# The FFN output projection as pairs of 64-row products in the PE array

## The chip, the core and the metric

The kernel runs on one core of a Trainium2 chip. The metric is the device time of one execution in microseconds (us); lower is better. Each compared time is the median of several executions, and beside them stands one profiled execution, whose trace is what the views of the profile are read from. Engines are named as the profile names them: PE is the matrix engine (PEld its weight loads), DVE and ACT the two engines that do elementwise work and activations, POOL a third one that here does little, and SP the engine that issues most DMAs.

## The reference

The program is a trunk of two layers on one sequence of 256 positions and 1024 channels, all in float32. Each layer has three sub-layers with an RMS norm before and after each: an FFN, a mixer (differential attention beside an mLSTM), and a second FFN. The change touches only the FFN:

```python
def _swiglu(h, w_in, w_out):
    gate, up = jnp.split(h @ w_in, 2, axis=-1)
    return (jax.nn.silu(gate) * up) @ w_out

h = _swiglu(_rmsnorm(x, g[0]), ffn_w_in[l, 0], ffn_w_out[l, 0])
x = x + 0.5 * _rmsnorm(h, g[1])
```

The hidden width is 2816. The input projection is 1024 by 5632, the output projection 2816 by 1024, and there are four FFNs in all.

## The kernel before

The 256 positions are two tiles `t` of 128 rows. The hidden width is cut into 11 chunks `c` of 256. For each chunk three weight pieces of 1 MB come from memory: two for the input projection and one, `wo`, for the output projection. Each half of a piece is split by ACT (line 278, the high part `wh`) and DVE (line 279, the low part `wl`), and a product in near-float32 precision is made of three PE products of the type fp32r: high by high, high by low, low by high (`mm3`, lines 393 to 395).

For a chunk and a tile, `in_piece` fills a PSUM bank `pin` with 24 such products of 128 rows of contraction, 128 stationary columns and 512 moving columns. `ffn_hidden` makes the hidden activations from it (ACT line 256, DVE line 516), `ffn_split` transposes them on PE (line 523, two transposes to a tile and chunk) and splits them into `hh` and `hl`. `out_part(c, t, h, wo)` then adds the chunk to the output: for each half `hf` of the 1024 output columns, 2 blocks `k` of 128 rows of contraction, by 3 products, 12 in all for a tile and chunk. The output of an FFN is held in four PSUM banks `bk`, one for each tile and column half, which are added to over all 11 chunks. So an FFN has 264 output products of 128 rows, and the four FFNs 1056.

The order on PE is set by a scheduler with a cost model, within the dependencies, except from `yield "ending"` (line 614) to `"running"`, where it is the order in which the code issues the instructions. Three chunks' outputs are still pending at the ending (`pend`). There the code issues: the transposes of tile 0 of the last chunk; the output of the oldest pending chunk for tile 0; the transposes of tile 1; the other two chunks for tile 0; `"done"` for tile 0, whose handler `postnorm` normalises the two finished banks and adds them to `x`; two chunks for tile 1; `"next"`, whose handler transposes the new `x` of tile 0 on PE for the next sub-layer (`prenorm`, line 412, 8 transposes); the last chunk for tile 1; and `"done"` for tile 1.

`postnorm` is a chain: ACT squares each bank with a running sum (line 454), DVE adds the two sums (line 438), POOL raises the sum to the power -1/2 (line 401), and DVE scales and adds to `x` in two halves (line 467).

Of the kernel before, what the change touches and what calls it, by code (L numbers as in the profile page):

```python
# [15 lines left out]
F32 = mybir.dt.float32  # L16
# [9 lines left out]
NT = S // P  # L26
# [29 lines left out]
def _pack(inp):  # L56
# [20 lines left out]
    for l in range(L):  # L77
        at = l * PIECES_LAYER
        ffn(at, l, 0)
        at += PIECES_FFN  # L80
        for n, lo in enumerate(MIX_GROUPS):
            a = m_in[l][:, lo:lo + 512].reshape(2, 4, P, 512).transpose(0, 2, 1, 3)
            w[at + 2 * n:at + 2 * n + 2] = a.reshape(2, P, 2048)
        at += 2 * len(MIX_GROUPS)
        w[at:at + 4] = m_out[l].reshape(4, 2, P, D).transpose(0, 2, 1, 3).reshape(4, P, 2048)
        ffn(at + 4, l, 1)
# [41 lines left out]
class _Trunk:  # L128
# [113 lines left out]
    def after(self, ins, others):  # L242

        for o in others:
            self.tc.add_manual_dep(ins.ins, o.ins.name, mybir.DependencyInfo(
                mybir.DependencyClass.NoSync, mybir.DependencyReason.DATA), reason="turn")

    def table(self, name, last=None):

        self.loaded = self.nc.scalar.preload_act_table_set(name)  # L250
        self.after(self.loaded, self.users + ([last] if last else []))
        self.users = []
# [280 lines left out]
    def ffn(self, pre, gi_post):  # L533
        xT, r = pre

        def in_piece(t, kh, pin, w):
            xh, xl = xT[t][kh]
            for k in range(4):
                self.mm3(pin, xh[:, k, :], xl[:, k, :], *self.cols(w, k),
                         start=kh == 0 and k == 0, stop=kh == 1 and k == 3)  # L540

        def out_part(c, t, h, wo):
            hh, hl = h[t]
            for hf in range(2):
                for k in range(2):
                    self.mm3(po[t][hf], hh[:, k, :], hl[:, k, :], *self.cols(wo, 2 * k + hf),
                             start=c == 0 and k == 0, stop=c == NC_FF - 1 and k == 1)

        po, pend = None, []
        if not xT:  # L550

            xT += [[], []]
            pins = [self.bank_bk() for _ in range(NT)]
            self.piece_at = 2
            with self.tc.manual_schedule(engines={mybir.EngineType.PE, mybir.EngineType.Activation, mybir.EngineType.DVE}):
                self.first_chunk(pins, xT)
            self.turns = [[(self.cast, self.split)]]
            for t in range(NT):
                ss = self.small("ss", (P, 2))
                for hf in range(2):  # L560
                    self.after(self.square(t, hf, ss), [self.cast])
                r.append(self.rsqrt_sum(ss, EPS))
            h = [self.ffn_evac(pins[t], r[t]) for t in range(NT)]
            begin = 1
        else:

            w0 = [self.piece(), self.piece()]
            w1 = [self.piece()]
            pa, pa1 = self.bank_pin(), self.bank_pin()
            in_piece(0, 0, pa, w0[0])  # L570
            in_piece(0, 1, pa, w0[1])
            ha = self.ffn_hidden(pa, r[0])
            yield "second"
            in_piece(0, 0, pa1, w1[0])
            ha = self.ffn_split(ha)
            pb = self.bank_pin()
            in_piece(1, 0, pb, w0[0])
            in_piece(1, 1, pb, w0[1])
            yield "running"
            w1.append(self.piece())  # L580
            in_piece(0, 1, pa1, w1[1])
            hb = self.ffn_evac(pb, r[1])
            pend = [(0, [ha, hb], self.piece())]
            pb1 = self.bank_pin()
            ha1 = self.ffn_evac(pa1, r[0])
            in_piece(1, 0, pb1, w1[0])
            in_piece(1, 1, pb1, w1[1])
            po = [[self.bank_bk() for _ in range(2)] for _ in range(NT)]
            for t in range(NT):
                out_part(0, t, *pend[0][1:])  # L590
            pend = []
            h = [ha1, self.ffn_evac(pb1, r[1])]
            begin = 2
        for c in range(begin, NC_FF):
            ws = [self.piece(), self.piece()]
            pend.append((c - 1, h, self.piece()))
            if c == 3:
                g = self.load_gpost(gi_post)
                yield "middle"
            pins = [self.bank_pin() for _ in range(NT)]  # L600
            for kh in range(2):
                for t in range(NT):
                    in_piece(t, kh, pins[t], ws[kh])
            if c == NC_FF - 1:
                break
            h = [self.ffn_evac(pins[t], r[t]) for t in range(NT)]
            if len(pend) == DEFER - 1 or po is None:
                if po is None:
                    po = [[self.bank_bk() for _ in range(2)] for _ in range(NT)]
                cc, hc, wo = pend.pop(0)  # L610
                for t in range(NT):
                    out_part(cc, t, hc, wo)

        yield "ending"
        h = [self.ffn_evac(pins[0], r[0]), None]
        pend.append((c, h, self.piece()))
        out_part(pend[0][0], 0, *pend[0][1:])
        h[1] = self.ffn_evac(pins[1], r[1])
        for p in pend[1:]:
            out_part(p[0], 0, *p[1:])  # L620
        yield "done", po[0], g
        for p in pend[:-1]:
            out_part(p[0], 1, *p[1:])
        yield "next"
        out_part(pend[-1][0], 1, *pend[-1][1:])
        yield "done", po[1], g


# [515 lines left out]
def _trunk(tc, a, out, phases=3 * L):  # L1144
    nc = tc.nc
    with contextlib.ExitStack() as st:
        def pool(name, bufs, **kw):
            return st.enter_context(tc.tile_pool(name=name, bufs=bufs, **kw))

        fill = pool("fill", 1)  # L1150
        fill.tile([P, FILL // 4], F32, name="fill")
        wr, wl, wh, trp, k4 = pool("wr", 3), pool("wl", 7), pool("wh", 7), pool("tr", 6), pool("k4", 6)
        hp, k2, const, ded = pool("hp", 4), pool("k2", 10), pool("const", 1), pool("ded", 1)
        const.tile([P, CFILL // 4], F32, name="cfill")
        pools = (const, wr, wl, wh, trp, k2, k4, ded, hp, pool("sm", 2), pool("ps", 1, space=PSUM))
        tr = _Trunk(tc, a, out, pools)
        tr.x = [tr.const.tile([P, D], F32, name=f"x{t}") for t in range(NT)]
        tr.early = {}
        tr.start()
        tr.users = []  # L1160
        tr.table("silu_and_others")
        tr.half = tr.const.tile([P, 16], F32, name="c_half")
        nc.gpsimd.memset(tr.half, -0.5)
        tr.run(phases)
# [17 lines left out]
```

## Time and profile before

| what | value |
|---|---|
| median of the runs shown | 985.39 us (985.11 to 985.68, 2 runs) |
| the profiled execution | 986.18 us, its span 984.4 us |
| PE busy | 976.0 us, 99% of the span |
| DVE, ACT, POOL busy | 606.4, 528.4 and 27.6 us |
| mean granted PE clock | 0.998 of full speed |
| memory traffic | 177.01 MB read, 181 GB/s over the span |

In the profile a row of a timeline gives the start, the duration, the engine, the line, the operation, the output and input by the program's names, the shape and the count; in brackets stands the idle time before it and what ended it. The shape `128*128 128x512` of a PE product is rows of contraction by stationary columns, then the moving operand. Products are pipelined, so that a PE product lasts longer (0.39 us) than the distance to the next one. The chain of waits gives each piece of work the time by which it put off the end.

### The profile page before, as it was taken

The numbers are of one execution on the slowest core, as the hardware profiler recorded it, in microseconds if no ns is written. First come the engines' busy times: TensorE is split into PE (matmuls) and PEld (weight loads), VectorE is DVE, ScalarE is ACT, GpSimd is POOL, SyncE is SP. The second block draws the span as 40 slices with busy tenths as digits, with TensorE's granted clock in tenths as the row PEclk, the third lists the DMA queues.
The fourth block names the chain that finished last, engine by engine and source line by source line (L and its number), as shares of the span: only waits on it lengthen the run. The fifth ranks groups of instructions, "written<-read, shape, count | busy, mean of one in ns | idle before, by whom it ended". The sixth has DMA issues, their size and how long they took to land.

```text
span 984.4 us, 12032 instructions
## 1 busy us (share of the span) xinstructions
PE 976.0 (99%) x4629; PEld 800.2 (81%) x4629; DVE 606.4 (62%) x863; ACT 528.4 (54%) x869; POOL 27.6 (3%) x51
## 2 busy tenths in 40 slices
PE   9999999999999999999999999999999999999997
PEld 6888888888788888888888888888888888888885
DVE  6755554589867655555485645455888586554542
ACT  7744444477856545444375544444778475544431
POOL 1000000000010000000000000000001000000000
PEclk9999999999999999999999999999999999999999
DMA  8954545336352844464356455443454257544511
GB/s 304 346 217 174 197 169 192 124 129 216 123 196 95 312 167 179 184 239 171 129 207 242 162 188 207 178 163 119 166 207 167 90 205 263 195 171 171 210 48 43
DMA packets 27640, 178.84 MB, mean 182 GB/s; under 512 B 3034, under 2 KB 4186, under 8 KB 6846
## 3 DMA queue, kind: packets, MB, share of 16 engines
q1 hardware_dynamic: 27006, 177.46, 48.9%
q8 instruction: 36, 0.59, 0.2%
q10 hardware_dynamic: 576, 0.61, 0.2%
q14 instruction: 22, 0.18, 0.0%
HBM read 177.01 MB, written 1.05 MB: 181 GB/s over the span
## 4 chain that ended last, share of the span: by engine, by line
PE 99%; DMA 1%; DVE 0%; SPq 0%; ACT 0%; POOLq 0%; issue 0%; DVEq 0%; ACTq 0%
PE pin L393 21%; PE pin L395 20%; PE pin L394 20%; PE bk L393 10%; PE bk L395 10%; PE bk L394 10%; PE ptr L523 2%; PE ptr L805 1%; PE ptr L412 1%; PE bk L1017 1%; PE bk L1057 1%; DMA x<-in_x_dram 1%; PE bk L372 0%; PE bk L370 0%; PE bk L1097 0%; PE bk L371 0%
## 5 line engine op out<-in xcount | busy, mean ns | idle before, releaser
L279 DVE TENSOR_TENSOR wl<-wr,wh 128x1024 fp32r<-128x1024 f32 x324 | 389.4, 1223 | 223.4 <-ACT wh L278 213.7
L278 ACT ACTIVATE wh<-wr 128x1024 fp32r<-128x1024 f32 x324 | 336.5, 1057 | 190.4 <-PE pin L395 102.1
L393 PE MATMUL pin<-wh,th 128*128 128x512 f32 x880 | 349.5, 398 | 0.0
L395 PE MATMUL pin<-wh,tl 128*128 128x512 f32 x880 | 343.4, 391 | 0.0
L394 PE MATMUL pin<-wl,th 128*128 128x512 f32 x880 | 343.3, 390 | 0.0
L395 PEld LDWEIGHTS pin<-wh,tl 128*128 128x128 f32 x880 | 165.2, 188 | 35.2
L393 PEld LDWEIGHTS pin<-wh,th 128*128 128x128 f32 x880 | 165.4, 188 | 33.3 <-ACT vd L1002 0.8
L394 PEld LDWEIGHTS pin<-wl,th 128*128 128x128 f32 x880 | 165.5, 188 | 32.3
L393 PE MATMUL bk<-wh,hh 128*128 128x512 f32 x352 | 140.0, 398 | 0.0
L395 PE MATMUL bk<-wh,hl 128*128 128x512 f32 x352 | 137.6, 393 | 0.0
L394 PE MATMUL bk<-wl,hh 128*128 128x512 f32 x352 | 137.6, 391 | 0.0
L526 ACT ACTIVATE hh<-ptr 128x256 fp32r<-128x256 f32 x88 | 33.2, 377 | 93.3 <-PE ptr L523 75.6
L256 ACT ACTIVATE sil<-pin,rs 128x256 f32<-128x256 f32 x86 | 40.5, 472 | 73.7 <-PE pin L395 69.8
L395 PEld LDWEIGHTS bk<-wh,hl 128*128 128x128 f32 x352 | 66.1, 188 | 13.8
L394 PEld LDWEIGHTS bk<-wl,hh 128*128 128x128 f32 x352 | 66.2, 188 | 12.8
L393 PEld LDWEIGHTS bk<-wh,hh 128*128 128x128 f32 x352 | 66.1, 188 | 12.8
L527 DVE TENSOR_TENSOR hl<-ptr,hh 128x256 fp32r<-128x256 f32 x88 | 37.1, 422 | 54.3 <-ACT hh L526 51.5
L516 DVE SCALAR_TENSOR_TENSOR h<-pin,rs,sil 128x256 f32<-128x256 f32 x86 | 41.2, 480 | 30.2 <-ACT sil L256 30.2
L401 POOL TENSOR_TENSOR rs<-s,c_half 128x1 f32<-128x1 f32 x24 | 13.1, 553 | 774.2 <-DVE s L438 774.2
L523 PEld LDWEIGHTS ptr<-c,h 128*128 128x128 f32 x176 | 24.7, 140 | 11.5
L523 PE MATMUL ptr<-c,h 128*128 128x128 f32 x176 | 33.4, 271 | 0.0
L454 ACT ACTIVATE junk<-bk 128x512 bf16<-128x512 f32 x24 | 14.2, 592 | 31.1 <-PE bk L395 31.1
(179 smaller groups left out, 586.8 us busy)
## 6 DMA issues: line engine op xcount, KB each, us to landing
wr<-in_w_dram SPq DMA_DIRECT2D x162, 1024.0 KB, 4.9
gpost<-in_gpost_dram SPq DMA_DIRECT2D x6, 512.0 KB, 6.2
wr<-in_w_dram SPq DMA_DIRECT2D x2, 512.0 KB, 7.1
wr<-in_w_dram SPq DMA_DIRECT2D x3, 256.0 KB, 5.2
x<-in_x_dram SPq DMA_DIRECT2D x3, 256.0 KB, 5.8
out_dram<-x SPq DMA_DIRECT2D x2, 256.0 KB, 2.1
x<-in_x_dram SPq DMA_DIRECT2D x2, 128.0 KB, 2.7
wr<-in_w_dram ACTq DMA_DIRECT2D x1, 256.0 KB, 3.5
```

The source lines that it names most:

```text
L256: i = self.nc.scalar.activation(*args, **kw)
L278: ia = nc.scalar.activation(hi, raw[:, j], AF.Copy)
L279: iv = nc.vector.tensor_tensor(lo, raw[:, j], hi.bitcast(F32), op=ALU.subtract)
L393: mm(ps, xh, wh, start=start, stop=False)
L394: mm(ps, xh, wl, start=False, stop=False)
L395: mm(ps, xl, wh, start=False, stop=stop)
L401: self.nc.gpsimd.tensor_tensor(r, ss, self.half[:, :width], op=ALU.pow)
L454: return nc.scalar.activation(self.junk_tile(), po[hf], AF.Square, scale=1.0 / (16 if half else 32), accum_out=ss[:, hf:hf + 1])
L516: nc.vector.scalar_tensor_tensor(h, pin[:, 256:512], r, sil, op0=ALU.mult, op1=ALU.mult)
L523: nc.tensor.transpose(ptr[:, k, :], h[:, k * P:(k + 1) * P], self.ident)
L526: nc.scalar.activation(hh, ptr, AF.Copy)
L527: nc.vector.tensor_tensor(hl, ptr, hh.bitcast(F32), op=ALU.subtract)
```

## The change

The 128 rows of contraction of each output product are cut into two halves of 64 rows. A product of the rows 0 to 63 stands in the upper half of the array and one of the rows 64 to 127 in the lower half, and the two that stand side by side belong to different PSUM banks. `rows_of` takes two orders of banks, one for each half of the array, issues the products of both in turn, and so each bank gets its upper and its lower half of the contraction at different times. Where a bank passes from one half of the array to the other, `behind` makes the first product there wait for the last one of the other half, by way of a one-element memset on POOL.

`out_rows` does this for a chunk with all four banks: the upper half of the array goes through tile 0 and then tile 1, the lower half through tile 1 and then tile 0. `out_tile` does it at the ending, for one tile with all three pending chunks: the upper half fills the bank of the first column half and then that of the second, the lower half the other way round. The ending changes with it: both tiles' last hidden activations are made and transposed first, then all of tile 0 follows, and `"next"` now stands before all of tile 1. The pool of `hh` and `hl` has six buffers in place of four.

```diff
+    def behind(self, ins, other):
+        step = self.nc.gpsimd.memset(self.sm.tile([1, 1], F32, tag="turn", name=self.name("turn")), 0.0)
+        for a, b in ((step, other), (ins, step)):
+            self.tc.add_manual_dep(a.ins, b.ins.name, mybir.DependencyInfo(
+                mybir.DependencyClass.Sync, mybir.DependencyReason.DATA), reason="turn")
...
+        def rows_of(orders):
+            for pair in zip(*orders):
+                for half, (t, hf, c, h, wo) in enumerate(pair):
+                    b, rows = 2 * t + hf, slice(half * 64, half * 64 + 64)
+                    for k in range(2):
+                        for lhs, rhs in ((0, 0), (0, 1), (1, 0)):
+                            todo[half].append((b, half, po[t][hf], h[t][lhs][rows, k, :], self.cols(wo, 2 * k + hf)[rhs][rows]))
+                for both in zip(*todo):
+                    for b, half, bank, x, w in both:
+                        i = self.nc.tensor.matmul(bank, x, w, start=last[b] is None, stop=False, skip_group_check=True)
+                        if last[b] and last[b][0] != half:
+                            self.behind(i, last[b][1])
+                        last[b] = half, i
+                for v in todo:
+                    v.clear()
+
+        def out_rows(c, h, wo):
+            p = (c, h, wo)
+            rows_of([[(t, hf, *p) for t, hf in order] for order in
+                     (((0, 0), (0, 1), (1, 0), (1, 1)), ((1, 0), (1, 1), (0, 0), (0, 1)))])
+
+        def out_tile(t, ps):
+            rows_of([[(t, hf, *p) for hf in order for p in ps] for order in ((0, 1), (1, 0))])
+
+        todo, last = [[], []], [None] * 4
...
-                for t in range(NT):
-                    out_part(cc, t, hc, wo)
+                out_rows(cc, hc, wo)
...
         h = [self.ffn_evac(pins[0], r[0]), None]
         pend.append((c, h, self.piece()))
-        out_part(pend[0][0], 0, *pend[0][1:])
         h[1] = self.ffn_evac(pins[1], r[1])
-        for p in pend[1:]:
-            out_part(p[0], 0, *p[1:])
+        out_tile(0, pend)
         yield "done", po[0], g
-        for p in pend[:-1]:
-            out_part(p[0], 1, *p[1:])
         yield "next"
-        out_part(pend[-1][0], 1, *pend[-1][1:])
+        out_tile(1, pend)
...
-        hp, k2, const, ded = pool("hp", 4), pool("k2", 10), pool("const", 1), pool("ded", 1)
+        hp, k2, const, ded = pool("hp", 6), pool("k2", 10), pool("const", 1), pool("ded", 1)
```

In the program's order the 1056 output products are now 2112 of 64 rows. They stand in 140 unbroken runs, and other PE work stands between the runs. In the changed kernel's line numbers, L570 is an output product of 64 rows, L400 to L402 are the products of `mm3`, L530 the transposes of the hidden activations, L419 those of `prenorm`, and L408 the power on POOL.

The first place is PE in the middle of the first FFN, after the output of a chunk for tile 0 (`bk_408` and `bk_409` are the banks of tile 0, `bk_410` and `bk_411` those of tile 1). Before:

```order
L394 MATMUL bk_409<-wl_1_462,hh_393 128x512
L395 MATMUL bk_409<-wh_1_463,hl_394 128x512
L523 MATMUL ptr_520<-c_95,h_518 128x128 x2
L393 MATMUL pin_616<-wh_0_541,th_126 128x512
L394 MATMUL pin_616<-wl_0_540,th_126 128x512
```

and now, at the end of a run and around the next one:

```order
L570 MATMUL bk_410<-wh_1_495,hl_405 128x512
L530 MATMUL ptr_713<-c_95,h_711 128x128 x2
L570 MATMUL bk_408<-wh_1_495,hl_394 128x512
L400 MATMUL pin_814<-wh_0_787,th_126 128x512
L401 MATMUL pin_814<-wl_0_786,th_126 128x512
L402 MATMUL pin_814<-wh_0_787,tl_127 128x512
L400 MATMUL pin_814<-wh_0_787,th_126 128x512
L401 MATMUL pin_814<-wl_0_786,th_126 128x512
L570 MATMUL bk_411<-wh_0_491,hh_404 128x512
L570 MATMUL bk_409<-wh_0_491,hh_393 128x512
```

Transposes and input products of 128 rows now stand between products of 64 rows, and the product into `bk_408` between them has lost its partner of the other half.

The second place is PE at the end of the first FFN, at `"next"`. Before, 24 output products of tile 1 (the last six of them are the first rows here) stand between the last one of tile 0 and the transposes of `x`:

```order
L393 MATMUL bk_411<-wh_0_1491,hh_1440 128x512
L394 MATMUL bk_411<-wl_0_1490,hh_1440 128x512
L395 MATMUL bk_411<-wh_0_1491,hl_1441 128x512
L393 MATMUL bk_411<-wh_1_1495,hh_1440 128x512
L394 MATMUL bk_411<-wl_1_1494,hh_1440 128x512
L395 MATMUL bk_411<-wh_1_1495,hl_1441 128x512
L412 MATMUL ptr_1657<-c_95,x_93 128x128 x4
L412 MATMUL ptr_1668<-c_95,x_93 128x128 x4
L393 MATMUL bk_410<-wh_0_1564,hh_1590 128x512
```

and now:

```order
L570 MATMUL bk_409<-wl_1_1879,hh_1869 128x512
L570 MATMUL bk_408<-wl_1_1879,hh_1869 128x512
L570 MATMUL bk_409<-wh_1_1880,hl_1870 128x512
L570 MATMUL bk_408<-wh_1_1880,hl_1870 128x512
L419 MATMUL ptr_1987<-c_95,x_93 128x128 x4
L419 MATMUL ptr_1998<-c_95,x_93 128x128 x4
L570 MATMUL bk_410<-wh_0_1637,hh_1546 128x512
L570 MATMUL bk_411<-wh_0_1637,hh_1546 128x512
```

The last products of both banks of tile 0 are now the instructions right ahead of the transposes of the `x` that is made from these banks, and all output products of tile 1 stand behind them.

The third place is POOL at the end of the first FFN, with the semaphores that each instruction waits for. Before, the powers of the two tiles' `postnorm` and of the next sub-layer's norms follow each other:

```order
L193 TENSOR_SCALAR c_570<-c_570 128x2
L401 TENSOR_TENSOR rs_177_1628<-s_176_1626,c_half 128x1 [waits DVE_49,Pool_49]
L401 TENSOR_TENSOR rs_192_1701<-s_191_1699,c_half 128x1 [waits DVE_49,Pool_49]
L401 TENSOR_TENSOR rs_197_1713<-s_196_1711,c_half 128x1 [waits DVE_49,Pool_49]
L401 TENSOR_TENSOR rs_214_1819<-s_213_1817,c_half 128x1 [waits DVE_49,Pool_49]
```

and now:

```order
L250 MEMSET turn_1933 1x1 [waits PE_49,Pool_49]
L250 MEMSET turn_1936 1x1 [waits Pool_49]
L250 MEMSET turn_2011 1x1 [waits Pool_49]
L408 TENSOR_TENSOR rs_240_1982<-s_239_1980,c_half 128x1 [waits DVE_49]
L250 MEMSET turn_2048 1x1 [waits PE_49,Pool_49]
L250 MEMSET turn_2051 1x1 [waits Pool_49]
L408 TENSOR_TENSOR rs_258_2097<-s_257_2095,c_half 128x1 [waits DVE_49]
```

Memsets that wait for PE now stand among the powers; the pair ahead of `rs_240` belongs to the change of banks inside tile 0, the pair behind it to that inside tile 1.

More of the change, by code (lines that the diff above doesn't have):

```diff
@@ L547, in out_part @@
                              start=c == 0 and k == 0, stop=c == NC_FF - 1 and k == 1)
+        last = [None] * 4
+        def rows_of(orders):
[20 more added lines that the diff above has]
+        todo, last = [[], []], [None] * 4
         po, pend = None, []
@@ L588, in ffn @@
             po = [[self.bank_bk() for _ in range(2)] for _ in range(NT)]
-            for t in range(NT):
-                out_part(0, t, *pend[0][1:])
+            out_rows(0, *pend[0][1:])
             pend = []
@@ L610, in ffn @@
                 cc, hc, wo = pend.pop(0)
-                for t in range(NT):
-                    out_part(cc, t, hc, wo)
+                out_rows(cc, hc, wo)
         yield "ending"
```

## The prediction

> **What bounds the kernel now.** First the profile's page: the span, PE's busy time, the chain of waits and the output products among the costliest groups.
>
> ```profile
> span 984.4 us, 12032 instructions
> PE 99%; DMA 1%; DVE 0%; SPq 0%; ACT 0%; POOLq 0%; issue 0%; DVEq 0%; ACTq 0%
> L393 PE MATMUL bk<-wh,hh 128*128 128x512 f32 x352 | 140.0, 398 | 0.0
> L395 PE MATMUL bk<-wh,hl 128*128 128x512 f32 x352 | 137.6, 393 | 0.0
> L394 PE MATMUL bk<-wl,hh 128*128 128x512 f32 x352 | 137.6, 391 | 0.0
> ```
>
> PE carries 99% of the chain. Whatever puts PE off puts off the end, and what the other engines do counts only where PE waits for it. The changed products are 3 x 352 = 1056. Their distance is read from a timeline of the first FFN's end: the first of these rows is the last output product of tile 0, the second stands 24 products on.
>
> ```profile
> 185.66 0.39 PE L395 MATMUL bk<-wh,hl 128*128 128x512 f32 x1
> ...
> 191.10 0.39 PE L395 MATMUL bk<-wh,hl 128*128 128x512 f32 x1
> ```
>
> (191.10 - 185.66) / 24 = 0.227 us: the output products cost 1056 x 0.227 = 240 us. Next I looked for 64-row products; the mixer has some. In the chain of waits (start, length of the piece, what):
>
> ```profile
> 247.19 1.09 PE bk L1017 x16
> 248.29 0.89 PE bk L972 x16
> 249.18 0.43 PE pin L393
> 249.61 0.23 PE pin L394
> ...
> 256.70 1.93 PE bk L1017 x16
> 258.63 0.43 PE pin L393
> 259.06 0.24 PE pin L394
> ...
> 270.55 2.68 PE bk L1057 x24
> ```
>
> L972 is 64 rows by 128 columns of plain float32, L1057 the same with 128 rows. 128 rows take 2.68 / 24 = 0.112 us each, 64 rows 0.89 / 16 = 0.056: two really run side by side, a pair in the time of one. But L1017 at 247.19 is as large as L972 and took 1.09, 0.20 more, and the first 128-row product behind each stretch took 0.43 where its neighbours take 0.23. So each change of shape costs PE 0.20 us, in both directions.
>
> **The change part by part.** *Pairs.* 1056 products become as many pairs at best. For two fp32r products of 512 columns side by side there is no row. Nearest in kind is the 128-row one at 0.227; nearest in shape are the L1017 pairs of 256 float32 columns, (1.93 - 0.20) / 8 = 0.216. I take 0.227, because every fp32r row shows it, output and input products alike (0.23 in the chain above), and keep 0.216 as the low end (and 0.233, as much above, for the high). At 0.227 side by side gains nothing by itself: the array did 128 rows in that time already.
>
> *Lost partners.* Walking the new order on PE, two halves each in turn, the 2112 half products need 1093 slots rather than 1056: where the scheduler split a run at an odd place, and in the first chunk of later FFNs, a product stands alone. 37 x 0.227 = 8.4 us.
>
> *Changes of shape.* The 2112 stand in 140 runs, with 128-row work on both sides: 140 x (0.20 + 0.20) = 56.0 us, all on PE. Ends: 0.15 each (14 us less), by the smaller stretches of the same chain, to 0.20.
>
> ```profile
> 262.95 0.59 PE bk L1086 x8
> 263.54 0.59 PE ptr L1049 x4
> ```
>
> (L1049 has 4 float32 products at 0.112 = 0.45, so 0.14 over.)
>
> *Turns on POOL.* In `out_rows` six pair slots (1.36 us) lie between the last product of a bank in one half and the first in the other, and the hand-over is shorter than that, so it is covered there. In `out_tile` nothing lies between: both halves swap banks at once. The trace has no such hand-over; its parts are the product's end, POOL's start behind DVE, a small memset and POOL's release:
>
> ```profile
> 3.27 0.11 POOL L239 MEMSET xpad<- 128x12 f32 x1
> ...
> 186.09 0.60 ACT L454 ACTIVATE junk<-bk 128x512 bf16<-128x512 f32 x1 [0.67 <-PE bk L395]
> 186.58 0.19 ACT L454 ACTIVATION_READ_ACCUMULATOR junk<-bk 128x1 f32 x1
> 186.81 0.16 DVE L438 SCALAR_TENSOR_TENSOR s<-ssp 128x1 f32<-128x1 f32 x1 [0.67 <-ACT junk L454]
> 187.12 0.57 POOL L401 TENSOR_TENSOR rs<-s,c_half 128x1 f32<-128x1 f32 x1 [141.83 <-DVE s L438]
> 187.72 1.41 DVE L467 SCALAR_TENSOR_TENSOR x<-tmp,rs,x 128x512 f32<-128x512 f32 x2 [0.15 <-POOL rs L401]
> ```
>
> 0.39 for the product, 0.15 to POOL (187.12 - 186.97), 0.11, 0.03 back, about 0.10 for weights that couldn't be loaded ahead (half a change of shape), less its slot of 0.227: 0.55 us. Two `out_tile` in four FFNs: 8 x 0.55 = 4.4 us (2 to 8). Queued behind those memsets on POOL is the power of the same tile's `postnorm`; it falls due later than they do, so that costs nothing.
>
> *Transposes of tile 1 at the ending.* They now stand right behind those of tile 0, with no output products between.
>
> ```profile
> 176.97 0.39 PE L395 MATMUL pin<-wh,tl 128*128 128x512 f32 x1
> 177.13 1.23 DVE L279 TENSOR_TENSOR wl<-wr,wh 128x1024 fp32r<-128x1024 f32 x1 [1.16 <-ACT wh L278]
> 177.20 0.38 PE L523 MATMUL ptr<-c,h 128*128 128x128 f32 x2
> 178.27 0.48 DVE L516 SCALAR_TENSOR_TENSOR h<-pin,rs,sil 128x256 f32<-128x256 f32 x1
> ```
>
> Their input is ready at 178.27 + 0.48 = 178.75, also held up by a weight split on DVE that stands ahead of it in the new order too. PE would be free at 177.20 + 2 x 0.109 = 177.42. With 0.03 for the release PE waits 1.36 us, four times: 5.4 us. All output products are queued behind this.
>
> *`"next"` ahead of tile 1.* Before, 24 products cover the chain from the last product of tile 0 to the new `x`. Now the cover is gone, and the chain is longer: both banks end together, so the first square (0.60 and 0.19, in step 0.68 us) no longer runs under the other bank's products. From the rows above: `x` in two parts, at 187.72 + 0.71 + 0.68 = 189.11 and 189.81. PE is free at 185.66 + 0.23 = 185.89, waits 3.25 us, does four transposes (0.44), waits 0.26 more: 3.51 us. Three FFNs have a successor: 10.5 us. At the end of the program the same extra square shows once: 0.7 us.
>
> *Larger pool, hidden activations earlier by a run:* nothing; in the new order the transposes inside an FFN still come 3.8 us or more after their bank's last product (counted in slots of 0.227), where the rows above need 1.8.
>
> Sum: 8.4 + 56.0 + 4.4 + 5.4 + 10.5 + 0.7 = 85.4 us. On the profiled 986.18 us that is 1071.6; the median lies 0.8 lower, at 985.39. Forecast: **1071 us**.
>
> **The rivals.** *Pairs at 0.216:* 1093 x 0.0115 = 12.6 less, 1058. For it: the L1017 rows. Against it: they are float32. 20%.
>
> *The clock falls in the waits at `"next"`.* The last product of the program ends at 977.67 + 0.39; then, by stretches (PE, PEld, DVE, ACT, POOL busy, PEclk):
>
> ```profile
> 977.67 0.39 PE L395 MATMUL bk<-wh,hl 128*128 128x512 f32 x1
> ...
> 978.00:981.00 3.00, 0.05 (x1) 0.00 (x0) 2.20 (x6) 0.69 (x2) 0.55 (x1) 1.00 0.00 0
> 981.00:982.00 1.00, 0.00 (x0) 0.00 (x0) 0.30 (x1) 0.00 (x0) 0.00 (x0) 0.68 0.65 240
> 982.00:984.00 2.00, 0.00 (x0) 0.00 (x0) 0.00 (x0) 0.00 (x0) 0.00 (x0) 0.50 0.43 142
> ```
>
> A mean of 0.68 means half clock from 981.36, after 3.3 us of idling. My wait of 3.25 us ends just under that. If it falls, products run at half speed until it is back; the program's start took about 4 us for that:
>
> ```profile
> 1.17 2.31 PE L382 MATMUL bk<-junk 128*128 128x512 bf16 x5 [1.17 <-DVE mp L906]
> ...
> 5.70 0.40 PE L371 MATMUL bk<-wh,tl 128*128 128x512 f32 x1
> ```
>
> Half of 4 us lost, three times: 6 us more, 1077. [...] 20%.
>
> *Two fp32r halves don't stream freely side by side.* The float32 pairs send half as many columns a microsecond (256 in 0.216), so they don't rule it out. Wholly one after the other: 2112 - 1093 slots more, 231 us, 1302; half of that, 1187. Then the change wouldn't do what it says. Against it: nothing in the L972 rows shows crowding. 12%. [...]
>
> *Not slower: the 0.20 is a weight load held by a wait, not the change of shape.* Then output products, whose operands have long been there, pay nothing between runs, and with weights loaded half by half they keep the L1017 pace: 1071 - 56 - 13 = 1002, within 2%. It decides if next to nothing of the toll is left, under 0.01 us at each of the 280 places. Against it: PEld ahead of 258.56 idles for nothing that the profile shows:
>
> ```profile
> 258.56 0.19 PEld L393 LDWEIGHTS pin<-wh,th 128*128 128x128 f32 x1 [0.33 <-issue]
> ```
>
> [...] 6%, and 2% for faster still.
>
> **How the numbers follow.** Forecast 40%, 0.216 pairs 20%, clock 20%, crowding 12%, the toll absent 6%, faster 2%. The range takes in the first three with the bounds of toll, pace and hand-over: down to 1058 - 14 = 1044, here 1046; up to 1077 + 6.6 (pairs at 0.233) + 3.6 (hand-over at 1 us) = 1087, with some for waits not seen, 1092. A change of 2% (965.7 to 1005.1) is about what a measurement here tells from none: faster 2%, same 6%, slower 92%.
>
> **What would show it.** Right: 64-row products in pairs 0.01 us apart, 0.22 to 0.23 us from pair to pair; the first product of a run and the first behind it 0.2 us late; PE idle 3.3 us ahead of the `prenorm` transposes and 1.4 ahead of tile 1's, released by DVE; 0.5 us by POOL inside each `out_tile`. Wrong: no late first products, pairs at 0.3 us or more, or waits for POOL inside `out_rows`.

## The result and the profile after

The changed kernel takes 1074.57 us (median of two, 1074.27 to 1074.87) where the kernel before takes 985.39. The ratio is 1.0905, with a 95% interval of 1.0858 to 1.0952: 9% slower, 89.2 us. The profiled execution took 1074.27 us.

First the profile's page of the changed kernel: the span, the share of each engine in the chain of waits, then the three groups of output products and one of their weight loads (busy us and mean ns of one, then the idle time ahead of them and what ended it).

```profile
span 1072.5 us, 14518 instructions
...
PE 97%; DVE 1%; issue 1%; ACT 1%; DMA 0%; POOL 0%; POOLq 0%; DVEq 0%; SPq 0%
...
L570 PE MATMUL bk<-wh,hh 64*128 64x512 f32 x704 | 162.2, 433 | 2.2 <-POOL turn L250 2.2
L570 PE MATMUL bk<-wh,hl 64*128 64x512 f32 x704 | 151.8, 395 | 0.0
L570 PE MATMUL bk<-wl,hh 64*128 64x512 f32 x704 | 148.3, 396 | 0.0
L570 PEld LDWEIGHTS bk<-wh,hh 64*128 64x128 f32 x704 | 71.4, 186 | 51.6 <-issue 30.1
```

Twice the products, and the groups together show 462 busy us where the three groups before showed 415: a pair takes the place of one product. PE still carries 97% of the chain. PE waited 2.2 us in all for POOL. The weight loads of the first kind of product stood idle for 51.6 us, most of it ended by "issue", which is a stop that no semaphore of the profile explains.

Where that stop lies is seen in a timeline of PE and PEld in the changed kernel, in the middle of the first FFN. A row with x2 is a pair whose two halves start together.

```profile
101.42 0.40 PE L400 MATMUL pin<-wh,th 128*128 128x512 f32 x1
101.75 0.19 PEld L570 LDWEIGHTS bk<-wh,hh 64*128 64x128 f32 x2 [0.36 <-issue]
101.75 0.50 PE L570 MATMUL bk<-wh,hh 64*128 64x512 f32 x2
101.86 0.19 PEld L570 LDWEIGHTS bk<-wl,hh 64*128 64x128 f32 x2
102.09 0.40 PE L570 MATMUL bk<-wl,hh 64*128 64x512 f32 x2
102.09 0.19 PEld L570 LDWEIGHTS bk<-wh,hl 64*128 64x128 f32 x2
102.32 0.40 PE L570 MATMUL bk<-wh,hl 64*128 64x512 f32 x2
...
103.02 0.40 PE L570 MATMUL bk<-wh,hl 64*128 64x512 f32 x2
103.35 0.50 PE L401 MATMUL pin<-wl,th 128*128 128x512 f32 x1
...
103.68 0.39 PE L402 MATMUL pin<-wh,tl 128*128 128x512 f32 x1
```

Within a run the weights of a pair load while the pair ahead of it is streaming (102.09 for the pair that starts at 102.32). At the change of shape they load only when the pair itself starts, 0.33 us behind the product ahead (101.42 to 101.75) in place of 0.23, and the next pair follows 0.34 us later (102.09). That is 0.10 + 0.11 us. On the way out it is the same: 0.33 to the first 128-row product, 0.33 to the one behind it. Why the weights of the other shape do not load earlier, the profile does not say.

The ending of the first FFN, PE alone: the transposes of tile 0 and of tile 1, the swap of banks inside tile 0's output, and the wait at `"next"` (this view ends at 205.5, ahead of the last of the eight transposes).

```profile
189.98 0.38 PE L530 MATMUL ptr<-c,h 128*128 128x128 f32 x2
191.59 0.44 PE L530 MATMUL ptr<-c,h 128*128 128x128 f32 x2 [1.23 <-DVE h L523]
191.95 0.50 PE L570 MATMUL bk<-wh,hh 64*128 64x512 f32 x2
...
195.94 0.39 PE L570 MATMUL bk<-wh,hl 64*128 64x512 f32 x2
196.60 0.53 PE L570 MATMUL bk<-wh,hh 64*128 64x512 f32 x2 [0.27 <-POOL turn L250]
196.94 0.42 PE L570 MATMUL bk<-wl,hh 64*128 64x512 f32 x2
...
200.60 0.40 PE L570 MATMUL bk<-wh,hl 64*128 64x512 f32 x2
204.11 1.73 PE L419 MATMUL ptr<-c,x 128*128 128x128 f32 x7 [3.10 <-DVE x L474]
```

The three steps that the prediction put there are there. Tile 1's transposes come 191.59 - 189.98 - 2 x 0.109 = 1.39 us late; over the four endings 1.39, 1.16, 1.39 and 1.03, 5.0 us. The swap costs (0.66 - 0.23) + (0.34 - 0.23) = 0.54 here, and as much at each of the eight. At `"next"` 3.51 us pass from the start of the last pair to that of the transposes of the new `x`, 3.28 beyond the pair's own slot; behind the other two waits PE stops for 0.2 us more between the fourth and the fifth transpose.

Behind that wait comes what the prediction had held to be a rival. Stretches of the changed kernel (busy us of PE, PEld, DVE, ACT and POOL with the number of instructions, then the granted PE clock, the DMA share and GB/s):

```profile
200.00:202.00 2.00, 1.01 (x10) 0.53 (x6) 0.24 (x1) 0.96 (x3) 0.00 (x0) 1.00 0.00 0
202.00:204.00 2.00, 0.00 (x0) 0.00 (x0) 1.91 (x5) 0.31 (x2) 0.57 (x1) 0.80 0.00 0
...
208.00:210.00 2.00, 2.00 (x14) 1.53 (x12) 0.17 (x1) 0.00 (x0) 0.00 (x0) 0.50 0.00 0
210.00:212.00 2.00, 2.00 (x20) 1.52 (x16) 0.00 (x0) 0.00 (x0) 0.00 (x0) 1.00 0.00 0
526.00:528.00 2.00, 1.01 (x6) 0.82 (x7) 1.78 (x3) 0.00 (x0) 0.03 (x1) 0.86 0.00 0
...
738.00:740.00 2.00, 1.46 (x8) 1.13 (x8) 1.72 (x3) 0.10 (x1) 0.00 (x0) 0.77 0.00 0
```

A mean of 0.80 over 202 to 204 is full clock until 203.2 and half from there, where pairs start 0.43 us apart in place of 0.23; it is back at 210.0. In the same way the clock fell at 527.5 and at 739.1, behind the other two waits, for 3.4 us each time.

### The profile page after: what moved, and what is told of

Its sections match the earlier page's. It is cut to its first block, busy times and chain, and to the rows that moved or that the text cites. A ratio compares the mean times of both kernels' runs of the same rounds, so it can differ in the third digit from the quotient of the medians.

```text
span 1072.5 us, 14518 instructions
## 1 busy us (share of the span) xinstructions
PE 1048.6 (98%) x5685; PEld 799.8 (75%) x5685; DVE 604.6 (56%) x863; ACT 528.5 (49%) x869; POOL 42.6 (4%) x315
## 4 chain that ended last, share of the span: by engine, by line
PE 97%; DVE 1%; issue 1%; ACT 1%; DMA 0%; POOL 0%; POOLq 0%; DVEq 0%; SPq 0%
PE bk L570 26%; PE pin L400 19%; PE pin L402 19%; PE pin L401 19%; PE ptr L530 3%; PE bk L400 1%; PE bk L401 1%; PE bk L402 1%; PE ptr L419 1%; PE ptr L837 1%; PE bk L1049 1%; PE bk L1089 0%; PE bk L379 0%; PE bk L377 0%; DVE wl L286 0%
## 5 line engine op out<-in xcount | busy, mean ns | idle before, releaser
L400 PE MATMUL pin<-wh,th 128*128 128x512 f32 x880 | 352.1, 400 | 0.0
L402 PE MATMUL pin<-wh,tl 128*128 128x512 f32 x880 | 346.3, 394 | 0.0
L402 PEld LDWEIGHTS pin<-wh,tl 128*128 128x128 f32 x880 | 165.2, 188 | 42.4 <-issue 8.7
L400 PEld LDWEIGHTS pin<-wh,th 128*128 128x128 f32 x880 | 165.4, 188 | 41.9 <-issue 10.1
L570 PE MATMUL bk<-wh,hh 64*128 64x512 f32 x704 | 162.2, 433 | 2.2 <-POOL turn L250 2.2
L570 PE MATMUL bk<-wh,hl 64*128 64x512 f32 x704 | 151.8, 395 | 0.0
L570 PE MATMUL bk<-wl,hh 64*128 64x512 f32 x704 | 148.3, 396 | 0.0
L570 PEld LDWEIGHTS bk<-wh,hh 64*128 64x128 f32 x704 | 71.4, 186 | 51.6 <-issue 30.1
L570 PEld LDWEIGHTS bk<-wh,hl 64*128 64x128 f32 x704 | 73.1, 187 | 16.2 <-issue 2.0
L570 PEld LDWEIGHTS bk<-wl,hh 64*128 64x128 f32 x704 | 71.6, 188 | 10.1 <-issue 1.3
L523 DVE SCALAR_TENSOR_TENSOR h<-pin,rs,sil 128x256 f32<-128x256 f32 x86 | 41.2, 480 | 28.6 <-ACT sil L263 28.6
L465 DVE TENSOR_TENSOR tmp<-bk,gpost 128x512 f32<-128x512 f32 x24 | 16.4, 687 | 53.5 <-ACT junk L461 53.5
L250 POOL MEMSET turn<- 1x1 f32 x264 | 15.9, 89 | 745.1 <-PE bk L570 745.0
L530 PEld LDWEIGHTS ptr<-c,h 128*128 128x128 f32 x176 | 19.3, 140 | 30.7 <-DVE h L523 12.8
```

Of the source, the lines that this page charges most:

```text
L400: mm(ps, xh, wh, start=start, stop=False)
L402: mm(ps, xl, wh, start=False, stop=stop)
L465: nc.vector.tensor_tensor(tmp[hf], po[hf], g[:, hf * 512:hf * 512 + 512], op=ALU.mult)
L523: nc.vector.scalar_tensor_tensor(h, pin[:, 256:512], r, sil, op0=ALU.mult, op1=ALU.mult)
L530: nc.tensor.transpose(ptr[:, k, :], h[:, k * P:(k + 1) * P], self.ident)
L570: i = self.nc.tensor.matmul(bank, x, w, start=last[b] is None, stop=False, skip_group_check=True)
```

## The experiments

Two questions were open: is the toll really the change of shape (and not hand-overs, crowding or late operands), and what is the new ending worth, with the clock's fall in it? The table gives all the runs; "64-row" counts the output products of 64 rows, "slots" the places that they take on PE.

| kernel | 64-row, runs, slots | median us | ratio to before (95%) |
|---|---|---|---|
| changed kernel | 2112, 140, 1093 | 1074.57 | 1.0905 (1.0858 to 1.0952) |
| the toll alone | 288, 119, 150 | 1038.22 | 1.0535 (1.0518 to 1.0553) |
| upper halves only | 768, 37, 768 | 998.02 | 1.0126 (1.0109 to 1.0143) |
| longer runs, 128 rows (control) | 0 | 984.68 | 0.9991 (0.9981 to 1.0000) |
| longer runs, old ending | 1536, 70, 787 | 1020.03 | 1.0354 (1.0338 to 1.0369) |
| the same, two memsets a hand-over | 1536, 70, 787 | 1021.15 | 1.0362 (1.0343 to 1.0381) |
| longer runs, new ending | 2112, 78, 1075 | 1050.21 | 1.0650 (1.0626 to 1.0673) |
| old ending | 1536, 132, 805 | 1046.28 | 1.0617 (1.0600 to 1.0635) |
| new ending, 128 rows | 0 | 1001.23 | 1.0160 (1.0145 to 1.0175) |
| `"next"` later | 2112, 140, 1093 | 1062.54 | 1.0781 (1.0765 to 1.0797) |
| wait filled, four FFNs | 2112, 141, 1093 | 1073.41 | 1.0890 (1.0874 to 1.0906) |
| wait filled, three FFNs | 2112, 140, 1093 | 1069.58 | 1.0852 (1.0836 to 1.0868) |

**The toll alone.** The edit to the kernel before, in `out_part`. `halves` issues the upper 64 rows of one column half and the lower 64 of the other, of the product `hl` by `wh` with `k` = 0; between its two calls stand the other ten products with 128 rows.

```diff
+            if 0 < c < NC_FF - 1:
+                one = halves(0)
+                for i, o in zip(one, two_of.get(t, ())):
+                    self.behind(i, o)
...
+                two = two_of[t] = halves(1)
+                for i, o in zip(two, one):
+                    self.behind(i, o)
+                return
```

> The kernel before, and in each of the nine middle chunks of an FFN one product (low half of the activations by high weights) of both column halves cut into two 64-row halves, so that two pairs of 64-row products stand between 128-row ones: 288 products of 64 rows in 119 runs and 150 slots instead of 144. All other output products keep their 128 rows, the ending is that of before, and the hand-overs on POOL lie far from where they are needed. Theory (each change of shape costs PE 0.20 us, in and out): 119 x 0.40 = 48 us, 6 lost partners 1.4 us, so 1033 to 1037 us. Rival (the toll is a weight load held by a late operand or a hand-over, not the change of shape): output products have their operands early and the hand-overs are done long before, so 985 to 990 us.

Measured: 1038.22, 52.9 us over before with one seventh of the changed kernel's 64-row products, and 1.2 above the expected range. The rival is out by 48 us. One such pair in this kernel's timeline of PE and PEld:

```profile
193.28 0.40 PE L568 MATMUL bk<-wh,hl 128*128 128x512 f32 x1
193.60 0.19 PEld L557 LDWEIGHTS bk<-wh,hl 64*128 64x128 f32 x2 [0.37 <-issue]
193.60 0.51 PE L557 MATMUL bk<-wh,hl 64*128 64x512 f32 x2
...
194.04 0.50 PE L400 MATMUL bk<-wh,hh 128*128 128x512 f32 x1
...
194.38 0.40 PE L401 MATMUL bk<-wl,hh 128*128 128x512 f32 x1
```

From 193.28 to 194.38 are 1.10 us where three products at 0.227 take 0.68: 0.42 for one pair between 128-row products. 119 x 0.42 + 1.4 = 51.4 of the 52.9, and 0.8 us of waiting for POOL come on top. The pair's operands lie in the same tiles as those of the 128-row products beside it, which had been used by then. So the toll needs no late operand, and it is slightly above the 0.40 that was expected.

**Upper halves only.** In the order of the next group, of each pair only the upper half is issued:

```diff
-                    for b, half, bank, x, w in both:
+                    for b, half, bank, x, w in both[:1]:
```

> The order with longer runs and the ending of before, and in the chunk loop only the upper half of each pair: the contraction rows 64 to 127 of the middle chunks are left out, so the output isn't the reference's. 768 products of 64 rows, each alone, in 37 runs; no hand-overs on POOL. Theory (a lone 64-row product takes the slot of a 128-row one, its partner in a pair is free, and the toll comes with the shape, not with pairing): 984.7 + 37 x 0.40 + 768 x 0.004 = 1002 us, 1000 to 1005, products 0.227 to 0.231 us apart, and the first of a run and the first behind it 0.20 us late as with pairs. Rival (pairs crowd each other, a lone one is faster): products closer than 0.22 us, under 995 us. Rival (the toll comes from two halves being loaded, not from the shape): no late first products, about 985 to 988 us.

Measured: 998.02, 2 us below the expected range, and neither rival. PE in this kernel, the end of a run and the beginning of the next:

```profile
99.70 0.39 PE L570 MATMUL bk<-wh,hl 64*128 64x512 f32 x1
100.01 0.66 PE L530 MATMUL ptr<-c,h 128*128 128x128 f32 x4
...
111.18 0.39 PE L402 MATMUL pin<-wh,tl 128*128 128x512 f32 x1
111.50 0.49 PE L570 MATMUL bk<-wh,hh 64*128 64x512 f32 x1
111.83 0.39 PE L570 MATMUL bk<-wl,hh 64*128 64x512 f32 x1
112.06 0.39 PE L570 MATMUL bk<-wh,hl 64*128 64x512 f32 x1
```

Single products pay the same 0.09 and 0.11 at the beginning of a run (111.18 to 111.50 to 111.83) and then stand 0.23 apart, as pairs do. So neither the second half nor its weights cost anything, and half the rows save nothing. The shortfall is mainly in the exits: 32 of these 37 runs end at transposes. There the first transpose comes 0.09 late (99.70 to 100.01) and the one behind it only 0.056 (0.165 in place of 0.109 in the trace), together 0.14 to 0.15 in place of 0.20. 37 x 0.20 + 32 x 0.145 + 5 x 0.20 = 13.0; measured 12.2 over before, 13.3 over the control of the next group. The 0.004 a product that was expected for the pace is not there either: these products stand 0.229 apart on average, 128-row products 0.228.

**Fewer runs.** The order on PE inside the chunk loop as the code writes it, in place of the scheduler's:

```diff
+            with self.tc.manual_schedule(engines={mybir.EngineType.PE}):
...
-                h = [self.ffn_evac(pins[t], r[t]) for t in range(NT)]
+                h = [self.ffn_hidden(pins[t], r[t]) for t in range(NT)]
...
                     out_rows(cc, hc, wo)
+                h = [self.ffn_split(v) for v in h]
```

The expectations call the runs unbroken; in the order as built most chunks' output still stands in two runs of 24, with input products between them, and the counts are of these. Three kernels have this order: with 128-row products and the old ending (the control), with pairs and the old ending, with pairs and the new ending.

> Control: the order of the unbroken runs in the chunk loop, the ending of before, and all output products of 128 rows; no pairs and no hand-overs on POOL. Every theory expects about the time of the kernel before, 983 to 992 us; what it has above 985.4 is the price of the fixed order alone and is taken off the unbroken runs.

> As the unbroken runs, but the ending of an FFN is that of before, with 128-row products: 1536 products of 64 rows in 70 runs, 787 slots instead of 768. To be read against the same order with 128-row products throughout (the control of this group). Theory: 70 x 0.40 + 19 x 0.227 + 787 x 0.004 (pairs were 0.231 us apart, 128-row products 0.227) = 35 us more than the control, about 1020 us; against the unbroken runs with the new ending 25 us less (the waits at the ending). Rival (the toll is not by run): no more than 10 us over the control.

> The changed kernel with the order on PE inside the chunk loop as the code writes it, so that the output products of a chunk stand in one unbroken run: 78 runs in place of 140, 1075 slots in place of 1093, the same products. Theory (toll for each change of shape): 62 x 0.40 + 18 x 0.227 = 29 us less, 1043 to 1049 us. Rival (the pairs themselves, or the hand-overs on POOL, make the loss): within 5 us of the changed kernel's 1074.6.

Measured: 984.68, 1020.03 and 1050.21. The fixed order costs nothing by itself. With pairs and the old ending it takes 35.35 us more than the control, where 35 was expected; 1.4 of them are a wait, told below, that was not. With the new ending 1050.21 is 24.4 less than the changed kernel, 4.6 short of the 29 that was expected and above the range; the rival is out.

The shortfall has two parts. With the old ending the longer runs save 26.3 (1046.28 to 1020.03), 2.6 less than 29: 27 of the exits saved led into transposes, 0.05 cheaper each, and in both of these kernels PE waits once in the first FFN for hidden activations (1.39 us with the old ending, 1.78 with the new), which neither the control nor the changed kernel shows there. What brings this wait is not shown. PE in the kernel with the new ending:

```profile
49.69 0.39 PE L402 MATMUL pin<-wh,tl 128*128 128x512 f32 x1
51.86 0.44 PE L530 MATMUL ptr<-c,h 128*128 128x128 f32 x2 [1.78 <-DVE h L523]
```

The other part is in the ending, which costs 30.2 here (25 was expected, for its waits) and 28.3 in the changed kernel. This difference of 1.9 fits the clock. Stretches of the kernel with the new ending:

```profile
514.00:516.00 2.00, 0.00 (x0) 0.00 (x0) 1.94 (x5) 0.28 (x2) 0.55 (x1) 0.85 0.00 0
516.00:522.00 6.00, 5.95 (x28) 4.76 (x30) 3.24 (x5) 1.26 (x2) 0.00 (x0) 0.50 0.00 0
522.00:524.00 2.00, 2.00 (x20) 1.57 (x16) 0.00 (x0) 0.00 (x0) 0.00 (x0) 0.95 0.00 0
```

Here the half clock lasts 6.8 us behind the second and the third wait (515.4 to 522.2, 720.2 to 727.0) and 3.4 behind the first: 17.1 us in all, 13.7 in the changed kernel. This kernel's own executions lay between 1045.8 and 1051.4, and the profiled one, at 1051.4, was the longest. The mean granted clock of the shortest one was 0.995, that of the profiled one 0.991: the shortest had less time at half clock. It has no trace.

**Longer hand-overs.** To the same order with the old ending, a second memset in each hand-over:

```diff
-        for a, b in ((step, other), (ins, step)):
+        more = self.nc.gpsimd.memset(self.sm.tile([1, 1], F32, tag="turn", name=self.name("turn")), 0.0)
+        for a, b in ((step, other), (more, step), (ins, more)):
```

> The unbroken runs with the ending of before, and every hand-over of a bank from one half of the array to the other by two chained one-element memsets on POOL in place of one: 240 hand-overs, each longer by a memset and its release, about 0.09 + 0.03 to 0.06 us, the same order on PE. Theory (inside a run of four banks the hand-over is covered by six slots of pairs, 1.36 us): within 1.5 us of the 1020.0 without the second memset. Rival (part of the loss is hand-overs that lie open in every run): 60 runs of 24 products with one open hand-over each, 7 to 9 us more, 1027 us or above.

Measured: 1021.15, 1.1 more than without (before was 0.3 longer in that comparison). Inside `out_rows` the hand-overs are covered: the rival had 7 to 9.

**The ending.** Three kernels: the changed kernel with the old ending; the new ending with 128-row products throughout; and the changed kernel with `"next"` moved:

```diff
         yield "done", po[0], g
+        out_tile(1, pend[:-1])
         yield "next"
-        out_tile(1, pend)
+        out_tile(1, pend[-1:])
```

> The changed kernel with the ending of before in 128-row products; the pairs stay in the middle of each FFN: 1536 products of 64 rows in 132 runs, 805 slots. It takes out of the changed kernel what the new ending brought: waits for tile 1's transposes 5.0, waits at the transposes of the new x 10.4, the stretches at half clock behind them 4, the swaps through POOL 4.0, the extra square 0.7, 8 changes of shape 3.2, 288 slots at the pair's pace 1.2: 28.5 us in all. Theory: 1044 to 1048 us. Rival (the ending costs only the idle time that its rows show, 15 us; the clock and the rest are nothing): 1058 to 1061 us. Rival (the whole loss sits in the ending): about 990 us.

> The changed kernel's code order and its new ending, with output products of 128 rows: no pairs, no changes of shape, no hand-overs on POOL. Theory: the ending's waits alone, 5.0 for the transposes of tile 1, 3 x 2.8 for those of the new x (the banks of tile 0 end one after the other here, so the first square runs under the second bank's products), at the program's end nothing: 998 to 1000 us, and up to 4 us more if the clock falls behind waits of 2.8 us as it did behind 3.4. Rival (only the 64-row shape costs): within 5 us of before's 985.4.

> The changed kernel with the transposes of the new x moved behind the first two of tile 1's three pending chunks, so that 24 slots of pairs (5.5 us) cover the chain of postnorm; slots and runs as before the move. Theory: the three waits of 3.4 to 3.5 us and the half-speed stretches behind them go, about 10.4 + 4; three more changes of shape in the middle of tile 1 (1.2) and four more swaps of banks through POOL with nothing between (2.0) come: 1060 to 1063 us, and a granted clock of full speed throughout. Rival (the clock's fall has another cause than these waits): 1064 to 1067 us, with half-clock stretches left.

Measured: 1046.28, 1001.23 and 1062.54. So the new ending costs the changed kernel 28.3 us, and the pairs in the middle the other 61.0. The ending's waits alone, without a single pair, cost 15.9 us, two falls of the clock included. Moving `"next"` behind the first two chunks of tile 1 brings 12.0 back, and there the clock reads 1.00 in every stretch of 5 us up to 1055, where PE's work is over. Each is what the first theory expected. In the kernel with 128-row products the wait at `"next"` is shorter, and the clock still fell at two of the three places. PE in its timeline at the first wait:

```profile
186.16 0.39 PE L566 MATMUL bk<-wh,hl 128*128 128x512 f32 x1
189.12 1.11 PE L419 MATMUL ptr<-c,x 128*128 128x128 f32 x5 [2.57 <-DVE x L474]
```

and stretches of the same kernel around the first wait and the third:

```profile
186.00:189.00 3.00, 0.55 (x3) 0.13 (x1) 1.54 (x4) 0.69 (x2) 0.57 (x1) 1.00 0.00 0
189.00:190.00 1.00, 0.84 (x5) 0.67 (x6) 0.85 (x2) 0.00 (x0) 0.00 (x0) 0.85 0.00 0
190.00:193.00 3.00, 3.00 (x10) 2.52 (x10) 2.46 (x4) 1.26 (x2) 0.00 (x0) 0.50 0.00 0
...
683.00:686.00 3.00, 0.68 (x4) 0.22 (x2) 1.43 (x4) 0.69 (x2) 0.55 (x1) 1.00 0.00 0
686.00:690.00 4.00, 3.74 (x20) 3.08 (x21) 3.45 (x6) 1.27 (x2) 0.00 (x0) 1.00 0.01 4
```

The first wait, 2.96 us from the last product to the transposes, is over at 189.12, and the clock falls at 189.7 all the same. The third, at 683, is as long to 0.03 us, and nothing falls.

**The clock.** To hold PE busy through the wait without changing what it waits for, three plain float32 products into a bank that nobody reads:

```diff
         yield "done", po[0], g
+        bank = self.bank_pin()
+        for _ in range(3):
+            self.nc.tensor.matmul(bank, self.ident, g[:, 0:512], start=True, stop=True)
         yield "next"
```

> The changed kernel with three plain float32 products of 128x512 into a bank that nobody reads, issued in each of the four FFNs between the last product of tile 0 and the transposes of the new x: they keep PE busy during the wait and take nothing from it. Theory (the idle time makes the clock fall, and half speed cost 4 us): no half-clock stretch in the trace, 4 us less, and up to 2.6 us more at the last FFN, which has no such wait: 1070 to 1073 us; in the three others the time from the last product of tile 0 to the transposes stays 3.4 to 3.5 us. Rival (the clock falls whatever PE does there, or its fall cost nothing): 1075 to 1078 us.

> The three plain float32 products of the filled wait again, but only in the three FFNs that have a successor, so that the last FFN pays nothing for them. Theory (idle PE in the waits makes the clock fall): the time lost to half speed, 5.5 us in the stretches from one wait to the next in the trace of the changed kernel, is saved: 1068 to 1070 us, full clock until the program's end. Rival (the fall cost nothing, or comes all the same): 1073 to 1076 us.

Measured: 1073.41 with the dummies in all four FFNs, 0.4 above the expected range; 1069.58 with them in three, 5.0 us below the changed kernel. Between the two are 3.8 us, where 2.6 were expected for the last FFN's dummies: they also cut a run of pairs in two there, 0.40 more for the toll, and the two medians have spreads of 0.6 and 1.5 us. PE in the timeline of the second, at the first wait (the three dummies, L658, stand as six records):

```profile
200.85 0.41 PE L570 MATMUL bk<-wh,hl 64*128 64x512 f32 x2
201.19 2.84 PE L658 MATMUL pin<-gpost,c 128*128 128x512 f32 x6
204.36 1.29 PE L419 MATMUL ptr<-c,x 128*128 128x128 f32 x8 [0.33 <-DVE x L474]
```

and stretches of the same kernel behind it:

```profile
204.00:206.00 2.00, 1.64 (x13) 1.21 (x14) 1.85 (x4) 0.25 (x1) 0.00 (x0) 1.00 0.00 0
```

The transposes still come 3.5 us behind the last product (200.85 to 204.36), so the wait is the same; the clock is full (1.00 in every stretch of 5 us up to 1060), and the time is 5.0 us shorter. So with PE busy through the wait the clock did not fall, and the falls behind idle PE cost about 5 us here.

## Why the prediction was right, and where it was off

The forecast of 1071 was 3.6 us short of 1074.57, and the sum of 85.4 us holds term by term, with one rival that came true beside it and one term that was left at nothing. That it came so close is in part luck: what the toll had too much, 3 us, made up for the pace, which had nothing and took 3.

| term | predicted us | shown us | by |
|---|---|---|---|
| changes of shape, 140 runs | 56.0 | 53 | the trace: 0.20 in, 0.20 out into input products (72), 0.15 into transposes (67) |
| lost partners | 8.4 | 8.4 | counted; inside the 61.0 of the middle |
| the pace of the pairs | 0 | 3 | the trace: 0.230 from pair to pair, 0.227 before |
| swaps in `out_tile` | 4.4 | 4.3 | eight times 0.54 in the trace |
| transposes of tile 1 | 5.4 | 5.0 | the trace, four endings |
| `"next"` | 10.5 | 10.2 | the trace: 3.28, 3.25 and 3.25 beyond the slot, twice 0.2 between the transposes |
| clock behind `"next"` | 0 (a rival, 6) | 5.0 | the filled wait |
| one more square | 0.7 | not measured by itself | |

With 0.7 for the square that is 89.6, against 89.2 measured. The middle can be checked alone: 132 runs at 0.38 (0.20 in, a mean of 0.18 out), 37 lost slots and 805 slots at 0.003 are 50.2 + 8.4 + 2.4 = 61.0 us, which is what the changed kernel with the old ending has over before. The ending's terms, with its share of toll (2.5) and pace (0.9), make 28.6 against the 28.3 measured.

*Pairs.* Side by side brings nothing, as argued: a pair takes the slot of one product. Between the two ends set for the unknown pace, 0.216 and 0.233, the value taken, 0.227, was 0.003 too low. The rival of 0.216 (by its own 0.011 a slot 12.0 us, not 12.6) and the crowding rival, whose lower price of 1187 us makes 0.33 us a pair, are both excluded: pairs stand 0.230 apart, and a lone half takes the same slot (0.229).

*Changes of shape.* The reading of the mixer's rows was right in cause and near in size, and the rival that explained the 0.20 by a held weight load is out by the kernel with the toll alone. The sum of 56.0 was 3 us too large: the exits into transposes are cheaper, which the sum had used as a lower end only (0.15, from the row of 0.59).

*The clock.* This is the step that failed: "My wait of 3.25 us ends just under that." The wait was as long as predicted, but the comparison with 3.3 us was the wrong test. In the traces the clock falls at moments of its own and not after a fixed time of idling, so the wait didn't have to be longer than 3.3: with 128-row products 2.96 us from product to transposes were enough at the first wait, where the fall came 0.6 us behind the wait's end, and 2.93 at the third were not. The rival's price, 6 us, was close to the 5.0 found. Its 4 us a fall were the author's estimate from the slow products at the program's start (0.58 to 0.63 us each), where the clock reads 1.00 all the same; the falls in the traces lasted 3.41 or 6.83 us. So 1071 was the sum without a loss that was in fact there. Its 5.0 us are more than the 3.6 that were missing, since toll and pace cancel and three small terms were up to 0.4 too large.

*The hand-overs* in `out_rows` are covered, as argued, and those in `out_tile` lie open, as argued too (0.27 us of idle PE at each).

## What to carry to other kernels

Cutting a product that fills the array into two halves side by side won nothing here (0.230 us a pair, 0.227 a whole product) and cost a toll of 0.35 to 0.42 us for each stretch of them; where small products are needed, keep them together, since the toll went by the number of stretches (52.9 us for 119 of them, 35.35 for 70). Before moving work away from a wait, look at what covers that wait: the last 24 products behind a normalisation were the cover here, and putting 24 slots of pairs back there won 12 us, about 5 of them (by the filled wait) from a clock that no longer fell afterwards. A toll that the trace shows elsewhere in the same program, at the same kind of place, can be multiplied out and come near: 56 us were forecast, 53 found.

## What was not expected of the hardware

In the traces of three kernels the clock's falls and returns stand on a grid. Read in stretches of 0.1 us, the three falls in the changed kernel's trace are at 203.19, 527.46 and 739.08 us, 324.27 and 211.62 apart: 95 and 62 times 3.413. In the kernel with 128-row products they are at 189.71 and 493.49, 89 times 3.413 apart, and in that with fewer runs and the new ending at 201.36, 515.38 and 720.18, 92 and 60 times; the step of 3.413 us is what these five distances give. Each fall lasted 3.41 or 6.83 us. A wait was then expensive here by where it fell on the grid, which lies elsewhere in each of these three traces. With 128-row products 2.96 us took the clock down at 186 and 2.93 us at 490, and 2.93 us did not at 683. Steps of that kernel's grid, ahead of the fall at 493.49 and in the wait at 683:

```profile
490.08:493.49 3.41, 0.87 (x6) 0.47 (x5) 1.98 (x4) 0.69 (x2) 0.55 (x1) 1.00 0.00 0
684.64:688.05 3.41, 1.79 (x11) 1.49 (x12) 3.13 (x5) 0.43 (x1) 0.55 (x1) 1.00 0.02 5
```

The wait at 683 is spread over two steps, in which PE is busy for 72% and 53% of the time; in the steps ahead of the eight falls of these three traces it was busy for 9 to 41%. So a step need not be wholly idle: between 199.78 and 203.19, the last step of the grid ahead of the first fall, PE was still busy for 1.2 us. Where the line between the two lies, no run here shows.
